# Start addresses of the fp32r operands in a decoder trunk: every one at a multiple of 64 bytes

## The chip, the cores and the metric

One core of one Trainium2 chip runs the whole program. The metric is the device time of one launch in microseconds. The kernel before takes 1127.47 us, the median of 3 runs (1127.37 to 1127.56).

## What is computed

A decoder trunk of two pre-RMSNorm layers on 512 tokens of width 1024, in float32. Cut to what matters here:

```
h = x
# layer 0
hn = rms_norm(h, mixer_norm_g[0])
q, k, v, g, u = split(hn @ w_in)              # 1024 -> 4 * 512 + 512
o = group_norm(retention(rope(q), rope(k), v))
h = h + concat([silu(g) * o, multiscale_pool(u)]) @ w_out
h = h + (silu(hf @ w_gate) * (hf @ w_up)) @ w_down     # hf = rms_norm(h), 1024 -> 2816 -> 1024
# layer 1
h = h + conformer_conv(rms_norm(h))           # 1024 -> 2 * 1024, GLU, causal conv of width 31,
                                              # LayerNorm, swish, 1024 -> 1024
h = h + swiglu(rms_norm(h))                   # as above
return rms_norm(h, final_norm_g)
```

## The kernel before, in words

The activations are kept feature major, as eight tiles of 128 features by 512 tokens. Every large product is made with three fp32r matmuls. Each operand is split into a part rounded to fp32r (the names end in h) and the exact rest (the names end in l), and `mm3` adds up high times high (L197), high times low (L198) and low times high (L199):

```
    def mm3(out, wh, wl, xh, xl, start, stop):
        nc.tensor.matmul(out, lhsT=wh, rhs=xh, start=start, stop=False)
        nc.tensor.matmul(out, lhsT=wh, rhs=xl, start=False, stop=False)
        nc.tensor.matmul(out, lhsT=wl, rhs=xh, start=False, stop=stop)
```

`lhsT` is the stationary operand, 128x128, loaded by a LDWEIGHTS of its own ahead of each matmul; `rhs` is the moving one, 128x512, or 128x256 where the tokens are worked in halves.

The weights come in 102 chunks of at most 128x2048 floats. `start_load` issues the transfer of a chunk to `wr`, and `split_load` makes `wh` on ScalarE (L179) and `wl` on VectorE (L182). Each of `wr`, `wh` and `wl` has two buffers, so chunk n+2 is written when TensorE is done with chunk n. `feature_major` runs over the eight feature tiles k of the input and over the two groups of 128 columns of a chunk, six matmuls for each k. `down` runs over the eleven hidden tiles f of half an FFN, three matmuls for each. For v and g (L446 to L448) the roles are exchanged: the activations are stationary and the weights move.

The stages on TensorE, with the name of the PSUM tile by which the profile knows each: `ps_qk`, `ps_u`, `ps_v`, `ps_g` (input projections), `ps_s` and `ps_o` (retention, in plain fp32), `ps_wo` (output projection), then `ps_gu` and `ps_dn` (the FFN's two products, each in two halves), `ps_pw` (the first product of the convolution module), `ps_c` (the convolution, plain fp32), `ps_p` (its last product; four small products of the pooling have that name too), and the second FFN. The last stage of the FFN, and parts of the convolution module, work in halves of 256 tokens.

The tiles lie in pools that are opened one after the other, and so their addresses in SBUF follow from the sizes of what was opened earlier: `const`, `res`, `wp` (weights), `xp` (the inputs `xgh`, `xgl` of `ps_gu` and `ps_pw`), `wk`, `sm` (small tiles, among them four for each tag of `rsqrt`, in two buffers), and, above all of them, one of `mx` (mixer), `hp` (hidden tiles `hh`, `hl` of an FFN) or `cx` and `cw` (convolution module). The first layer's inputs `xgh`, `xgl` lie in `mx`, as do `mh` and `ml`; `zh` and `zl` lie in `cx`.

Of the kernel before, what the change touches and what calls it, by code (L numbers as in the profile page):

```python
# [34 lines left out]
# columns of the per-channel vectors packed as [128, n]  # L35
# [8 lines left out]
# columns of the constants that depend on shapes alone  # L44
# [7 lines left out]
# 2*pi cut into parts: products with the rounded quotients are exact  # L52
# [5 lines left out]
def _parts(bits, n):  # L58
    # 2*pi to 120 bits
    num = 0x6487ED5110B4611A62633145C06E0E68  # L60
    den = 1 << 124
    out = []
    from fractions import Fraction
    rest = Fraction(num, den)
    for _ in range(n):
        e = 0
        while rest >= Fraction(2) ** (e + 1):
            e += 1
        while rest < Fraction(2) ** e:
            e -= 1  # L70
        unit = Fraction(2) ** (e - bits + 1)
        part = (rest // unit) * unit
        out.append(float(part))
        rest -= part
        if rest == 0:
            break
    return out
# [3 lines left out]
def trunk(ctx: ExitStack, tc: tile.TileContext, a: dict):  # L81
# [14 lines left out]
    vg = const.tile([P, KT], F32, name="vg")  # L96

# [15 lines left out]
    # TensorE's clock rises while it is busy: products of zeros until the first data arrive  # L113
# [6 lines left out]
    # ---------------------------------------------------------------- weights  # L120
# [16 lines left out]
    def start_load():  # L137
        """The transfer of the next chunk of weights."""
        i = state["started"]
        if i >= len(plan):  # L140
            return
        state["started"] += 1
        name, j, kt, c = plan[i]
        raw = wp.tile([P, CHUNK], F32, tag="wr", name=f"wr{i}", bufs=AHEAD + 1)
        if i == 0:
            # the first rows of x and of the weights arrive side by side
            for k in range(KT):
                s = slice(k * c, (k + 1) * c)
                nc.sync.dma_start(X[:, k, :], xT[k])
                nc.sync.dma_start(raw[:, s], a[name][j][:, s])  # L150
            nc.sync.dma_start(con, a["con"])
        else:
            pieces = 4 if i == 1 else 1
            step = kt * c // pieces
            for k in range(pieces):
                s = slice(k * step, (k + 1) * step)
                nc.sync.dma_start(raw[:, s], a[name][j][:, s])
        raws[i] = raw

    def split_load(pieces=1, apart=False):  # L160
        """The split of the next chunk of weights: one step per piece, or two."""
        i = state["next"]
        if i >= len(plan):
            return
        if i not in raws:
            start_load()
        state["next"] += 1
        name, j, kt, c = plan[i]
        n = kt * c
        raw = raws.pop(i)  # L170
        wh = wp.tile([P, CHUNK], F32R, tag="wh", name=f"wh{i}")
        wl = wp.tile([P, CHUNK], F32R, tag="wl", name=f"wl{i}")
        ready[(name, j)] = (wh[:, :n].rearrange("p (k c) -> p k c", c=c),
                            wl[:, :n].rearrange("p (k c) -> p k c", c=c))
        pieces = KT if i == 0 else 4 if i == 1 else pieces
        step = n // pieces
        for k in range(pieces):
            s = slice(k * step, (k + 1) * step)
            nc.scalar.copy(wh[:, s], raw[:, s])  # L179
            if apart:  # L180
                yield
            nc.vector.tensor_tensor(wl[:, s], raw[:, s], wh[:, s].bitcast(F32), ALU.subtract)  # L182
            if i == 0:
                norm_input(k, vg[:, k:k + 1], None, xin)
            yield
# [15 lines left out]
    def feature_major(ps, wh, wl, xh, xl, cols=FULL, between={}, ks=range(KT)):  # L201
        """ps[:, i] = the i-th 128 columns of the weights, transposed, times x; between: what else is issued, and when."""
        for k in ks:
            if k in between:
                between[k]()
            for i in range(2):
                c = slice(i * P, (i + 1) * P)
                mm3(ps[:, i, cols], wh[:, k, c], wl[:, k, c], xh[k][:, cols], xl[k][:, cols], k == 0, k == KT - 1)

    def high_first(ps, wh, wl, xh, xl, cols, ks):  # L210
        """feature_major, without xl as long as it can be."""
        for low in range(2):
            for k in ks:
                for i in range(2):
                    c = slice(i * P, (i + 1) * P)
                    o = ps[:, i, cols]
                    if low:
                        nc.tensor.matmul(o, lhsT=wh[:, k, c], rhs=xl[k][:, cols], start=False, stop=k == KT - 1)
                    else:
                        nc.tensor.matmul(o, lhsT=wh[:, k, c], rhs=xh[k][:, cols], start=k == 0, stop=False)  # L220
                        nc.tensor.matmul(o, lhsT=wl[:, k, c], rhs=xh[k][:, cols], start=False, stop=False)

    def split_scaled(h, l, src, scale):
        """h + l = src * scale, h rounded to 12 significant bits, l the exact rest."""
# [7 lines left out]
    # -------------------------------------------------------------- residual  # L232
# [7 lines left out]
    def norm_input(k, gain, acc, pool=None):  # L240
        """The split of X[k] * gain, and X[k]^2 added to acc."""
# [15 lines left out]
    def rsqrt(v, n, tag):  # L257
        """v ** -0.5 on [128, n], by Newton steps from the exponent's halving."""
        y = sm.tile([P, n], F32, tag=f"rs_y{tag}", name="rs_y")
        t = sm.tile([P, n], F32, tag=f"rs_t{tag}", name="rs_t")  # L260
        hv = sm.tile([P, n], F32, tag=f"rs_h{tag}", name="rs_h")
        half = sm.tile([P, n], I32, tag=f"rs_i{tag}", name="rs_i")
# [9 lines left out]
    def token_sums(acc, cols=FULL):  # L272
        """Sums over the partitions: [128 tokens, tiles of tokens]."""
# [7 lines left out]
    def spread(v, name, out=None):  # L281
        """[128 tokens, n] -> [128, 128 n], the same row on every partition."""
# [21 lines left out]
    def add_residual(j, ps, gain=None, acc=None, bias=None):  # L304
        """X of tiles 2j and 2j+1 += ps, then the next norm's input."""
# [18 lines left out]
    # ------------------------------------------------------- retention + pool  # L324
    def mixer():
        nonlocal xin
        with ExitStack() as m:
# [4 lines left out]
            # both halves of the partitions share the angles: one half of the tokens on each  # L332
# [18 lines left out]
            # rotary tables  # L351
# [11 lines left out]
            # the last rounding can leave the range by an ulp  # L363
# [12 lines left out]
            # q and k, rotated  # L376
# [27 lines left out]
            # pooling, feature major  # L404
            def pool_group(gi, ps):
# [5 lines left out]
                while d < w:  # L411
                    # columns before the first stay zero in u: windows reach back w - 1 at most
# [43 lines left out]
            # scores, transposed: [keys, queries]; heads' outputs token major  # L456
# [16 lines left out]
            # normalised in place of v  # L473
# [27 lines left out]
            # the pooled half of the output projection, then the gated heads, back to feature major  # L501
# [22 lines left out]
    # ------------------------------------------------------------------- FFN  # L524
# [4 lines left out]
    def ffn_in(layer, acc, gain, hp):  # L529
        nacc = None  # L530
        row = {}
        for half in range(2):
            hh, hl = [], []

            def hidden(ps):
# [5 lines left out]
                hh.append(hp.tile([P, S], F32R, tag="hh", name=f"hh{len(hh)}"))  # L541
                hl.append(hp.tile([P, S], F32R, tag="hl", name=f"hl{len(hl)}"))
# [30 lines left out]
    def finish(hh, hl, acc):  # L573
        """The last two tiles, and the last norm with the tokens on the partitions, in halves of the tokens."""
# [6 lines left out]
        def tail_add(i, cols):  # L581
            """The residual, its square and its product with the gain."""
# [7 lines left out]
        def turn(t, ks):  # L590
            """Tiles ks of x to rows of tokens."""
# [48 lines left out]
    # ------------------------------------------------------------------ conv  # L640
    def conv(acc):
        with ExitStack() as m:
# [12 lines left out]
            def gated(j, ps, cols, between=lambda: None):  # L655
                """u of tile j, after CW columns of zeros."""
# [13 lines left out]
                # R[32 q + c, i, t] = u[4 c + i, t + q]  # L670
                if j not in Rs:
                    Rs[j] = cw.tile([P, 4, 28 + S], F32, tag="R", name=f"R{j}")
                    # taps of 32 channels, four at a time, on the diagonals
# [31 lines left out]
            # Channels less a pivot, the mean of two of the tiles: their sums and those of their squares  # L705
            # give the mean and the variance, which the pivot's distance from the mean cannot swamp.
# [14 lines left out]
            def pivot_tile(j, ps, cols):  # L721
                """A convolved tile, with its bias and less the pivot, into the sums."""
# [8 lines left out]
            def stats(cols):  # L731
                """The mean less the pivot and the reciprocal deviation: [128 tokens, 2]."""
# [69 lines left out]
            # the last tiles and the norm in halves of the tokens: each engine's work in this order  # L802
# [85 lines left out]
def _chunks(w, cols, kt=None):  # L888
    """(K, M) -> [chunk, 128, kt * cols]: columns cut first, then rows."""
# [7 lines left out]
def _paired(a, b):  # L897
    """Columns of a and b, 128 of one beside 128 of the other."""
    K, M = a.shape
    return np.stack([a.reshape(K, M // P, P), b.reshape(K, M // P, P)], 2).reshape(K, 2 * M)  # L900
# [69 lines left out]
```

## Time and profile before

| | |
|---|---|
| median of 3 runs | 1127.47 us |
| span of the profiled execution, first to last instruction | 1125.3 us |
| TensorE (PE) busy | 1110.1 us, 99% |
| weight loads (PEld) busy | 896.5 us, 80% |
| VectorE (DVE) busy | 579.8 us, 52% |
| ScalarE (ACT) busy | 334.9 us, 30% |
| granted TensorE clock, mean | 0.997 |

The profiled execution has no device time of its own beside its span; 2.2 us of the median lie around the span. A profile's row gives engine, operation, output and inputs, shapes, and the number of instructions. A matmul's duration in these rows is longer than the distance from its start to the start of the next one, since matmuls overlap in the array; where this text speaks of a pitch, it means that distance from start to start. A timeline row begins with the start in microseconds and the duration.

### The profile page before, as it was taken

Reading aid. Unit: us, or ns where it says so; the run is one execution under the profiler, and the core shown is the slowest. Engines: PE = TensorE matmul, PEld = TensorE weight load, DVE = VectorE, ACT = ScalarE, POOL = GpSimd, SP = SyncE. Lnnn points to the kernel's source line nnn. Section 1 sums busy time; section 2 is a strip of 40 time slices with the busy share of each in tenths; the row PEclk is TensorE's granted clock in tenths of the full one; section 3 lists DMA queues with packets and bytes.
Section 4 is the critical chain, followed back from the end, with each engine's and each line's share of the span. In section 5 each row is a group of like instructions: output and inputs, shape, how many; then the busy total and the mean of one; then the engine's idle time right before and its main releaser. Section 6 shows DMA issues by size and latency. Waiting matters only on the chain.

```text
span 1125.3 us, 12874 instructions
## 1 busy us (share of the span) xinstructions
PE 1110.1 (99%) x5504; PEld 896.5 (80%) x5504; DVE 579.8 (52%) x784; ACT 334.9 (30%) x383; POOL 20.1 (2%) x10
## 2 busy tenths in 40 slices
PE   9999999999999999999999999999999999999996
PEld 6877778888888888888886577988888888888886
DVE  7876636453432343534569957854444324344333
ACT  6631134232221232323322124432322112222231
POOL 0000100000000000000000410000000000000000
PEclk9999999999999999999999999999999999999998
DMA  8322113222223323222427562233222232231212
GB/s 278 123 85 103 38 38 119 107 81 107 78 78 126 112 75 112 76 77 91 139 86 117 93 141 76 75 113 111 77 101 67 88 133 92 101 112 52 96 59 75
DMA packets 24744, 109.89 MB, mean 98 GB/s; under 512 B 2800, under 2 KB 6768, under 8 KB 15984
## 3 DMA queue, kind: packets, MB, share of 16 engines
q1 hardware_dynamic: 24112, 108.03, 29.7%
q8 instruction: 43, 0.70, 0.3%
q10 hardware_dynamic: 576, 1.05, 0.3%
q14 instruction: 13, 0.11, 0.0%
HBM read 100.34 MB, written 2.10 MB: 91 GB/s over the span
## 4 chain that ended last, share of the span: by engine, by line
PE 91%; DVE 6%; ACT 1%; DMA 1%; issue 1%; SPq 0%; DVEq 0%; ACTq 0%
PE ps_gu L197 14%; PE ps_gu L198 14%; PE ps_gu L199 14%; PE ps_dn L199 7%; PE ps_dn L198 7%; PE ps_dn L197 7%; DVE d L692 4%; PE ps_c L700 2%; PE ps_qk L198 1%; PE ps_qk L197 1%; PE ps_wo L198 1%; PE ps_qk L199 1%; PE ps_wo L199 1%; PE ps_wo L197 1%; PE ps_pw L197 1%; PE ps_pw L198 1%
## 5 line engine op out<-in xcount | busy, mean ns | idle before, releaser
L179 ACT CAST wh<-wr 128x2048 fp32r<-128x2048 f32 (+4 forms) x116 | 179.7, 1553 | 517.0 <-PE ps_gu L198 240.5
L197 PE MATMUL ps_gu<-xgh,wh 128*128 128x512 f32 x704 | 274.4, 390 | 0.0
L198 PE MATMUL ps_gu<-xgl,wh 128*128 128x512 f32 x704 | 273.9, 389 | 0.0
L199 PE MATMUL ps_gu<-xgh,wl 128*128 128x512 f32 x704 | 273.9, 389 | 0.0
L182 DVE TENSOR_TENSOR wl<-wr,wh 128x2048 fp32r<-128x2048 f32 (+4 forms) x116 | 214.1, 1849 | 104.5 <-ACT wh L179 104.2
L538 DVE TENSOR_TENSOR gu<-ps_gu,bc_rms 128x1024 f32<-128x1024 f32 x44 | 53.9, 1224 | 210.9 <-PE ps_gu L199 202.8
L199 PEld LDWEIGHTS ps_gu<-xgh,wl 128*128 128x128 f32 x704 | 132.1, 188 | 27.8
L197 PEld LDWEIGHTS ps_gu<-xgh,wh 128*128 128x128 f32 x704 | 132.1, 188 | 27.3
L198 PEld LDWEIGHTS ps_gu<-xgl,wh 128*128 128x128 f32 x704 | 132.2, 188 | 27.2
L199 PE MATMUL ps_dn<-hh,wl 128*128 128x512 f32 (+1 forms) x374 | 144.1, 385 | 0.0
L198 PE MATMUL ps_dn<-hl,wh 128*128 128x512 f32 (+1 forms) x374 | 142.4, 381 | 0.0
L197 PE MATMUL ps_dn<-hh,wh 128*128 128x512 f32 (+1 forms) x374 | 142.3, 380 | 0.0
L198 PEld LDWEIGHTS ps_dn<-hl,wh 128*128 128x128 f32 x374 | 70.3, 188 | 16.1
L197 PEld LDWEIGHTS ps_dn<-hh,wh 128*128 128x128 f32 x374 | 70.2, 188 | 14.9
L199 PEld LDWEIGHTS ps_dn<-hh,wl 128*128 128x128 f32 x374 | 70.2, 188 | 14.3
L197 PE MATMUL ps_pw<-xgh,wh 128*128 128x512 f32 (+1 forms) x160 | 56.3, 352 | 0.0
L229 ACT CAST hh<-act 128x512 fp32r<-128x512 f32 x44 | 27.3, 621 | 96.5 <-DVE act L540 96.5
L198 PE MATMUL ps_pw<-xgl,wh 128*128 128x512 f32 (+1 forms) x160 | 55.6, 347 | 0.0
L199 PE MATMUL ps_pw<-xgh,wl 128*128 128x512 f32 (+1 forms) x160 | 55.5, 347 | 0.0
L308 DVE TENSOR_TENSOR X<-ps_dn,X 128x1024 f32<-128x1024 f32 x15 | 18.4, 1225 | 69.7 <-PE ps_dn L199 69.7
L230 DVE TENSOR_TENSOR hl<-act,hh 128x512 fp32r<-128x512 f32 x44 | 30.5, 693 | 30.2 <-ACT hh L229 30.2
L700 PE MATMUL ps_c<-R,dg 128*32 128x512 f32 (+1 forms) x512 | 42.9, 487 | 2.3 <-ACT d L751 1.3
(188 smaller groups left out, 1184.7 us busy)
## 6 DMA issues: line engine op xcount, KB each, us to landing
wr<-in_w_gu SPq DMA_DIRECT2D x44, 1024.0 KB, 4.8
wr<-in_w_dn SPq DMA_DIRECT2D x32, 704.0 KB, 4.0
wr<-in_w_pw SPq DMA_DIRECT2D x12, 1024.0 KB, 4.9
R<-u SPq DMA_DIRECT2D x16, 270.0 KB, 8.5
wr<-in_w_o SPq DMA_DIRECT2D x4, 1024.0 KB, 4.7
X<-in_xT SPq DMA_DIRECT2D x8, 256.0 KB, 4.5
wr<-in_w_qk SPq DMA_DIRECT2D x2, 1024.0 KB, 5.4
wr<-in_w_u SPq DMA_DIRECT2D x2, 1024.0 KB, 4.8
```

Source lines behind the costliest of these rows:

```text
L179: nc.scalar.copy(wh[:, s], raw[:, s])
L182: nc.vector.tensor_tensor(wl[:, s], raw[:, s], wh[:, s].bitcast(F32), ALU.subtract)
L197: nc.tensor.matmul(out, lhsT=wh, rhs=xh, start=start, stop=False)
L198: nc.tensor.matmul(out, lhsT=wh, rhs=xl, start=False, stop=False)
L199: nc.tensor.matmul(out, lhsT=wl, rhs=xh, start=False, stop=stop)
L229: nc.scalar.copy(h, src)
L230: nc.vector.tensor_tensor(l, src, h.bitcast(F32), ALU.subtract)
L308: nc.vector.tensor_tensor(xx, ps, xx, ALU.add)
L538: nc.vector.tensor_tensor(t, ps, both(row["rb"]), ALU.mult)
L692: nc.vector.scalar_tensor_tensor(o, us[j][:, at], V("dwc", CW * j + q), o, ALU.mult, ALU.add)
L700: nc.tensor.matmul(ps[32 * i:32 * i + 32, :n], lhsT=dgs[j][:, i, g, :], rhs=Rs[j][:, i, 4 * g + cols.start:4 * g + cols.stop], start=g == ...
```

## The change

It alters where tiles lie, and nothing else. Tiles `wh` and `wl` become 64 bytes longer per partition, and so do the hidden tiles `hh` and `hl`, of which the first 512 columns are used as before. A 64-byte tile `pad` in `const` moves all later pools by 64 bytes. Four tiles of `rsqrt` have one buffer in place of two for the tag "b", and `rs_i` for "a4" too, which makes room and moves the pools above `sm`.

```diff
+ODD = 16
+PAD = 2
...
+    pad = const.tile([P, 8 * PAD], F32, name="pad") if PAD else None
...
-        wh = wp.tile([P, CHUNK], F32R, tag="wh", name=f"wh{i}")
-        wl = wp.tile([P, CHUNK], F32R, tag="wl", name=f"wl{i}")
+        wh = wp.tile([P, CHUNK + ODD], F32R, tag="wh", name=f"wh{i}")
+        wl = wp.tile([P, CHUNK + ODD], F32R, tag="wl", name=f"wl{i}")
...
-        y = sm.tile([P, n], F32, tag=f"rs_y{tag}", name="rs_y")
-        t = sm.tile([P, n], F32, tag=f"rs_t{tag}", name="rs_t")
-        hv = sm.tile([P, n], F32, tag=f"rs_h{tag}", name="rs_h")
-        half = sm.tile([P, n], I32, tag=f"rs_i{tag}", name="rs_i")
+        y = sm.tile([P, n], F32, tag=f"rs_y{tag}", bufs=1 if tag == "b" else 2, name="rs_y")
+        t = sm.tile([P, n], F32, tag=f"rs_t{tag}", bufs=1 if tag == "b" else 2, name="rs_t")
+        hv = sm.tile([P, n], F32, tag=f"rs_h{tag}", bufs=1 if tag == "b" else 2, name="rs_h")
+        half = sm.tile([P, n], I32, tag=f"rs_i{tag}", bufs=1 if tag in ("b", "a4") else 2, name="rs_i")
...
-                hh.append(hp.tile([P, S], F32R, tag="hh", name=f"hh{len(hh)}"))
-                hl.append(hp.tile([P, S], F32R, tag="hl", name=f"hl{len(hl)}"))
+                hh.append(hp.tile([P, S + ODD], F32R, tag="hh", name=f"hh{len(hh)}")[:, :S])
+                hl.append(hp.tile([P, S + ODD], F32R, tag="hl", name=f"hl{len(hl)}")[:, :S])
```

The instructions of every engine, their order and their waits are the same in both programs, row for row; line numbers grow by up to four. What differs is the addresses. From the programs as built, the start of each fp32r operand within its partition, modulo 128 bytes (the column and row steps inside a tile are multiples of 128 bytes, so one number stands for a whole tile):

| stage | fp32r matmuls of 512 columns | moving, before | stationary, before | moving, after | stationary, after |
|---|---|---|---|---|---|
| `ps_gu` | 2112 | 64 | 64 | 0 | 0 or 64 by chunk |
| `ps_pw` | 288 (and 192 of 256 columns) | 64 | 64 | 0 | 0 or 64 by chunk |
| `ps_dn` | 990 (and 132 of 256) | 32 | 64 | 64 or 0 by tile | 0 or 64 by chunk |
| `ps_p`, last product | 96 (and 192 of 256) | 32 | 64 | 64 | 0 or 64 by chunk |
| `ps_qk` and `ps_u` | 192 and 96 | 32 | 64 | 64 | 0 or 64 by chunk |
| `ps_wo` | 192 | 32, half of them 96 | 64 | 64, half of them 0 | 0 or 64 by chunk |
| `ps_v` and `ps_g` | 96 and 96 | 64 | 32 | 0 or 64 by chunk | 64 |
| `ps_p`, pooling | 12 | 96 | 96 | 0 | 0 |

So after the change about half of the 512-column matmuls have both operands at the same place modulo 128, and the other half have them 64 bytes apart. Pools `wp` and `xp` lie between 35,520 and 117,440 bytes, `mx`, `hp` and `cx` begin at 139,808 (before) or 139,840 (after).

## The prediction

> **What bounds the kernel now.** The page comes first: the engines' busy time, and the chain of work that ended last.
>
> ```profile
> span 1125.3 us, 12874 instructions
> ...
> PE 1110.1 (99%) x5504; PEld 896.5 (80%) x5504; DVE 579.8 (52%) x784; ACT 334.9 (30%) x383; POOL 20.1 (2%) x10
> ...
> PE 91%; DVE 6%; ACT 1%; DMA 1%; issue 1%; SPq 0%; DVEq 0%; ACTq 0%
> ```
>
> PE is busy nearly all the time and makes up 91% of the chain. "Busy" alone does not say that it works at its best, so the view of waits follows, for PE alone, and the busy time by stage, with the cuts laid where the product changes.
>
> ```profile
> PE ps_ms L278 <- DVE acc L761: 1.5, 1, 1.5
> ```
>
> ```profile
> 312.20:373.80 61.60, 61.60 (x266) 49.55 (x264) 19.74 (x14) 12.82 (x11) 0.00 (x0) 1.00 0.30 106
> 373.80:493.50 119.70, 119.70 (x529) 99.10 (x528) 50.96 (x42) 32.06 (x31) 0.00 (x0) 1.00 0.26 91
> ```
>
> The longest wait of PE on another engine is 1.5 us in the whole span (the view lists the longest first: total, times, longest one). In the FFN's stages (the two rows of the second view; columns are length, then PE, PEld, DVE, ACT, POOL) PE has no gap, the clock column reads 1.00, DVE is busy for 32% (19.74 of 61.60) and 43% (50.96 of 119.70). There only the pitch of the matmuls counts, the distance from one start to the next. The first row is one half of an FFN's `ps_dn`: 8 chunks of 33 matmuls, 264, in 61.60 us, 233.3 ns each. The second is `ps_gu`: 11 chunks of 48, 528, in 119.70 us, 226.7 ns each. (The counts in brackets take in neighbours that overlap an edge.) Same width, same clock, no wait, and 6.7 ns apart. The timeline of PE gives the pitch elsewhere, from the first and last row of a stretch without a gap:
>
> ```profile
> 724.63 0.39 PE L197 MATMUL ps_p<-zh,wh 128*128 128x512 f32 x1
> ...
> 735.83 0.39 PE L197 MATMUL ps_p<-zh,wh 128*128 128x512 f32 x1
> 39.78 0.40 PE L198 MATMUL ps_qk<-xgl,wh 128*128 128x512 f32 x1
> ...
> 50.28 0.40 PE L198 MATMUL ps_qk<-xgl,wh 128*128 128x512 f32 x1
> 53.78 0.40 PE L198 MATMUL ps_u<-xgl,wh 128*128 128x512 f32 x1
> ...
> 64.98 0.40 PE L198 MATMUL ps_u<-xgl,wh 128*128 128x512 f32 x1
> 169.83 0.40 PE L198 MATMUL ps_wo<-ml,wh 128*128 128x512 f32 x1
> ...
> 180.79 0.40 PE L197 MATMUL ps_wo<-mh,wh 128*128 128x512 f32 x1
> 125.80 0.39 PE L448 MATMUL ps_g<-wh,xgl 128*128 128x512 f32 x1
> ...
> 136.80 0.40 PE L447 MATMUL ps_g<-wl,xgh 128*128 128x512 f32 x1
> ```
>
> There are 48, 45, 48, 47 and 47 steps between the two rows of each pair: 233.3 ns for `ps_p`, `ps_qk` and `ps_u`, 233.2 for `ps_wo`, 234.0 for `ps_g`. So there are two classes, and the table of addresses sorts them without an exception. Where both operands begin at 64 modulo 128 (`ps_gu`, and `ps_pw`, which runs the same code as `ps_gu`), the pitch is 226.7. Where the moving operand lies at 32 or 96, or the stationary one at 32 (`ps_g`), it is 233.2 to 234.0. Code and shapes don't sort them: `ps_qk`, `ps_p` and `ps_gu` all come out of `feature_major` with the same steps, and the first layer's `xgh` in `mx` is slow where its namesake in `xp` is fast.
>
> Narrow matmuls show no difference. First `ps_pw` of 256 columns, all at 64, then `ps_dn` of 256, whose moving operand is at 32:
>
> ```profile
> 663.75 0.28 PE L198 MATMUL ps_pw<-xgl,wh 128*128 128x256 f32 x1
> ...
> 668.43 0.28 PE L198 MATMUL ps_pw<-xgl,wh 128*128 128x256 f32 x1
> 1099.74 0.28 PE L199 MATMUL ps_dn<-hh,wl 128*128 128x256 f32 x1
> ...
> 1102.86 0.28 PE L198 MATMUL ps_dn<-hl,wh 128*128 128x256 f32 x1
> ```
>
> 39 steps in 4.68 us and 26 in 3.12: 120.0 ns both. From this and 226.7, 256 more columns cost 106.7 ns, so 512 columns by themselves would take 213.3, and 13.3 ns of each aligned matmul are no streaming.
>
> **The change part by part.** The order and the waits are the same, so no term comes from a moved instruction. The counts, one row of each stage (its other two lines have as many):
>
> ```profile
> L197 PE MATMUL ps_gu<-xgh,wh 128*128 128x512 f32 x704 | 274.4, 390 | 0.0
> L197 PE MATMUL ps_dn<-hh,wh 128*128 128x512 f32 x330 | 129.4, 392 | 0.0
> L197 PE MATMUL ps_pw<-xgh,wh 128*128 128x512 f32 x96 | 37.7, 393 | 0.0
> L197 PE MATMUL ps_qk<-xgh,wh 128*128 128x512 f32 x64 | 25.7, 402 | 0.0
> L446 PE MATMUL ps_g<-wh,xgh 128*128 128x512 f32 x32 | 13.1, 411 | 0.0
> ```
>
> The 390 ns in the first row is not the pitch: a matmul's end lies behind the start of the next.
>
> 1. `ps_dn`: 990 x 6.67 ns = 6.60 us. I take 226.7 for the new pitch, the row of the only wide fp32r matmuls with both operands at multiples of 64.
> 2. `ps_p` of 512 columns, 96 x 6.67 = 0.64 us, and `ps_u`, 96 x 6.67 = 0.64 us.
> 3. `ps_wo`, 192 x 6.67 = 1.28 us. The short waits of its stage stay.
> 4. `ps_qk`: 192. The first chunk of 48 runs while x arrives and I count it at nothing; 144 x 6.67 = 0.96 us. All of them would be 1.28.
> 5. `ps_v` and `ps_g`: 192 x (234.0 - 226.7 = 7.3) = 1.41 us.
> 6. `ps_gu` and `ps_pw`, 2112 + 288 matmuls: 0. They were aligned to 64 and still are, but the moving operand goes from 64 to 0 modulo 128, and every second chunk has its operands 64 bytes apart. No row of this trace has that. From both sides: it cannot save more than the 13.3 ns that are no streaming, and a cost of as much again, 13.3, is my upper estimate, twice the 6.7 that a distance of 32 costs.
> 7. Matmuls of 256 columns, plain fp32 ones, the 12 of the pooling: 0, by the rows of 120.0 ns; the 12 are under 0.1 us at 6.7 ns each.
> 8. `rsqrt` with fewer buffers: 0. Its tiles are written and read on DVE, in order, and no wait is added.
>
> On the path all of this is PE's own time, so it counts in full as long as the next chunk comes in time. `ps_dn` is the tightest, 33 matmuls for a chunk, 7.70 us now and 7.48 after:
>
> ```profile
> L182 DVE TENSOR_TENSOR wl<-wr,wh 128x1408 fp32r<-128x1408 f32 x32 | 52.0, 1625 | 58.4 <-ACT wh L179 58.4
> ...
> L179 ACT CAST wh<-wr 128x1408 fp32r<-128x1408 f32 x32 | 44.0, 1374 | 178.0 <-PE ps_dn L198 122.4 <-PE ps_gu L198 47.9 <-issue 7.7
> ```
>
> ```profile
> wr<-in_w_dn SPq DMA_DIRECT2D x32, 704.0 KB, 4.0
> ```
>
> The transfer of 4.0 us, the rounding of 1.37 and the rest's 1.63 are steps of a pipeline, none near 7.48, and ScalarE waits for PE, not PE for it. That cover would have to shrink by over 4 us a chunk before a gap opened. With the 6.7 ns gone, nothing else is late.
>
> The sum: 6.60 + 0.64 + 0.64 + 1.28 + 0.96 + 1.41 = 11.53 us off the profiled span of 1125.3, 1113.8. The median of the runs, 1127.47, stands 2.2 us above that span, for what lies around it; with the same 2.2 the forecast is 1115.9.
>
> A rule of the Trainium skill speaks against term 5. "TensorE: Matmul & The Clock Gate", Part 2, step 1, says that PE has two independent SBUF read ports, and that loading the next weights takes no read bandwidth from the running matmul. By it a stationary operand's address could not show in the pitch while its load is hidden, and term 5 would be 0 (sum 10.1, 1117.3). The trace disagrees: the loads take as long in both stages,
>
> ```profile
> L197 PEld LDWEIGHTS ps_gu<-xgh,wh 128*128 128x128 f32 x704 | 132.1, 188 | 27.3
> L447 PEld LDWEIGHTS ps_g<-wl,xgh 128*128 128x128 f32 x32 | 6.0, 189 | 1.5
> ```
>
> 188 and 189 ns, hidden in 226.7 and 234.0, and yet `ps_g`, with its moving operand at 64 and only its stationary one at 32, is slow. I keep the term.
>
> **The rivals.**
>
> *A. Operands 64 bytes apart free each other.* `ps_g` shows that the two streams of reads affect one another, so part of the 13.3 ns may be reads that meet at the same place modulo 128, where every fast row of before has both operands. If the half of the 4158 wide fp32r matmuls that now has them apart lost 6.67 ns more, 2079 x 6.67 = 13.9 us would come on top: 1102.0. With all 13.3 ns gone, 27.7 us: 1088.2. Against it: the trace has no wide matmul under 226.7.
>
> *B. The distance is what costs.* 0 bytes apart is 226.7, 32 apart is 233.3 (either operand), 96 against 64 is 233.2. These rows fit "each operand off a multiple of 64" as well as "the operands apart". If 64 apart costs what 32 does, 1200 matmuls of `ps_gu` and `ps_pw` lose 6.67 (8.0 us) and half of the 11.53 us, 5.8, does not come: 1115.9 + 8.0 + 5.8 = 1129.7. If it grows with the distance, to 240.0, `ps_gu` and `ps_pw` lose 1200 x 13.33 = 16.0 us, and of the 1758 slow ones half gain and half lose 6.67: 1127.5 + 16.0 = 1143.5. This is the case on the other side: it decides from 11.53 us / 2079 = 5.5 ns per matmul 64 apart, and passes 0.2% slower, 2.25 us, at 6.6 ns. That bound of 0.2% is about what a measurement of this kernel can tell from no change. It ends on the slower side because more matmuls would leave the good place than reach it. Against it: a distance of 32 costs 0 in the narrow rows.
>
> *C. It is not the alignment.* Every slow stage has an operand in the pools above 139,808 bytes (`mx`, `hp`, `cx`), every fast one has both below. If the region matters, the change does nothing: 1127.5. Against it: `ps_g` and `ps_qk` come to nearly the same pitch with the operand up there in the other role, and no term in the trace depends on how far up it lies. A page bears on it: the Trainium skill's "SBUF — State Buffer", section "Door 1", speaks of 16-byte lines, and 32, 64 and 96 are all multiples of 16, so by that line size no operand gains by moving. The two classes of pitch do not look like it, unless C holds.
>
> *D. Only a part comes,* because the moving operand must be at 64 and not at 0 modulo 128, or the like: half of 11.53, 1121.7.
>
> **How the numbers follow.** The forecast, all alignment to 64 and nothing of 128, has 0.55: 1115.9. A has 0.16, D 0.05, C 0.10, B 0.14 (0.09 at 1129.7, 0.05 at 1143.5). Faster by over 0.2%: the forecast, A and D, 0.76. Within 0.2%: C and half of B's first value, 0.14. Slower: the rest of B, 0.10. The range goes from A's first value less a microsecond, 1101, to C plus one, 1128.5; left out are B and the far end of A, no more than 0.2.
>
> **What would show it.** In the profile after: a half of `ps_dn` takes 59.8 us in place of 61.60, 226.7 ns a matmul; a half of `ps_gu` still 119.7; wide matmuls of `ps_qk`, `ps_u`, `ps_wo`, `ps_p`, `ps_v`, `ps_g` all at 226.7; narrow ones at 120.0; PE's waits as they were. Wrong, and A or B, if pitches of neighbouring chunks of `ps_gu` differ, down or up; C if `ps_dn` stays at 233.3. A wait of PE for `wh` or `wl` in `ps_dn` would make the sum wrong though the pitches are right.

## The result, and the profile after

The changed kernel takes 1135.44 us (median of 4 runs, 1135.16 to 1135.84) against 1127.45 of the kernel before beside it. The ratio is 1.007, with a 95% interval of 1.0056 to 1.0084: slower, where 1115.9 was forecast. The profiled execution's span grew from 1125.3 to 1133.7 us.

The page of the kernel after, the same lines as before:

```profile
span 1133.7 us, 12874 instructions
...
PE 1119.6 (99%) x5504; PEld 897.8 (79%) x5504; DVE 579.9 (51%) x784; ACT 334.3 (29%) x383; POOL 19.7 (2%) x10
...
PE 95%; DVE 3%; ACT 1%; issue 1%; DMA 0%; SPq 0%; DVEq 0%; ACTq 0%
```

PE's busy time grew by 9.5 us and the others' stayed. The longest waits of PE show no new one:

```profile
PE ps_c L704 <- ACT d L755: 1.4, 1, 1.4
PE ps_idle L122 <- DVE zero L119: 1.2, 1, 1.2
```

So it is the pitch. The stages that were shown of before, a half of `ps_dn` and then a half of `ps_gu`, each cut at the start of its first matmul and of the next stage's first (length, PE busy, clock, share of DMA, GB/s):

```profile
314.07:375.37 61.30, 61.30 (x265) 1.00 0.30 106
375.37:497.66 122.29, 122.29 (x529) 1.00 0.26 89
```

`ps_dn` went from 61.60 to 61.30 us where 59.8 was forecast, 232.2 ns a matmul. `ps_gu`, which was to stay at 119.7, went to 122.29, 231.6 ns. There are two such halves of `ps_gu` in each FFN, +2.6 us for this one and about 10 us for all four; that is more than the whole loss. Two neighbouring chunks of `ps_gu`, of which the second has its weights in the other pair of buffers:

```profile
375.37:386.49 11.12, 11.12 (x49) 1.00 0.34 119
386.49:397.61 11.12, 11.12 (x50) 1.00 0.26 96
```

Both take 11.12 us for 48 matmuls. Rival B, as it was written, has one chunk at 226.7 and its neighbour slow; here both are slow by the same amount, though in one of them every operand begins at 0 modulo 128.

That is where the new theory came from. In the kernel before, the fast stages had more in common than the place modulo 128: their operands lay at the same place modulo 512 too, by the pool's sizes. In what follows, a distance is the start of a matmul's moving operand less that of its stationary one, in bytes, taken modulo 256 unless it is said otherwise; the starts are those of the built programs. Theory D (D for distance; it is not the prediction's rival D) says that the pitch depends on the distance alone. It began with a period of 512, and `scan32` brought it to 256. The kernel before has distance 0 in `ps_gu` and `ps_pw`, 96 in `ps_dn`, `ps_qk`, `ps_u`, the last product's `ps_p` and half of `ps_wo`, 32 in the other half, and 160 in `ps_v` and `ps_g`. The kernel after has, in `ps_gu`, 0 to `wh` and 128 to `wl` in one chunk, 192 and 64 in the next.

### The profile page after: what moved, and what is told of

Read it like the earlier page. It is cut to its first block, busy times and chain, and to the rows that moved or that the text cites. A ratio compares the mean times of both kernels' runs of the same rounds, so it can differ in the third digit from the quotient of the medians.

```text
span 1133.7 us, 12874 instructions
## 1 busy us (share of the span) xinstructions
PE 1119.6 (99%) x5504; PEld 897.8 (79%) x5504; DVE 579.9 (51%) x784; ACT 334.3 (29%) x383; POOL 19.7 (2%) x10
## 4 chain that ended last, share of the span: by engine, by line
PE 95%; DVE 3%; ACT 1%; issue 1%; DMA 0%; SPq 0%; DVEq 0%; ACTq 0%
PE ps_gu L203 14%; PE ps_gu L202 14%; PE ps_gu L201 14%; PE ps_dn L201 7%; PE ps_dn L203 7%; PE ps_dn L202 7%; PE ps_pw L201 2%; PE ps_pw L203 2%; PE ps_pw L202 2%; PE ps_c L704 2%; DVE d L696 2%; PE ps_wo L202 1%; PE ps_qk L202 1%; PE ps_wo L203 1%; PE ps_qk L203 1%; PE ps_qk L201 1%
## 5 line engine op out<-in xcount | busy, mean ns | idle before, releaser
L203 PE MATMUL ps_gu<-xgh,wl 128*128 128x512 f32 x704 | 278.8, 396 | 0.0
L202 PE MATMUL ps_gu<-xgl,wh 128*128 128x512 f32 x704 | 277.2, 394 | 0.0
```

## The experiments

The kernels are built on before, except `no_odd`. The first four ran on one chip, beside the same runs of before (1128.2 us).

**One place for all, `one_class`.** The pool `sm` is shrunk to 1536 bytes, and a tile of 320 bytes goes in ahead of `pwh`; all fp32r operands then begin at 192 modulo 512. Besides the smaller `rsqrt` tiles of the change:

```diff
-        v = sm.tile([P, NT], F32, tag="ms", name="ms")
+        v = sm.tile([P, NT], F32, tag="ms", name="ms", bufs=1)
...
-        v = sm.tile([P, 2], F32, tag="ms2", name="ms")
+        v = sm.tile([P, 2], F32, tag="ms2", name="ms", bufs=1)
...
+            mx.tile([P, 80], F32, name="mpad")
             pwh = mx.tile([P, 4, P], F32R, name="pwh")
```

> Before, with the pools shifted so that both operands of every fp32r matmul begin at 192 modulo 512. Theory D (the pitch is 226.7 ns when moving and stationary operand begin at the same place modulo 512, whatever that place is, and some 231 to 236 otherwise): every wide stage at 226.7, narrow ones at 120.0, about 1116 us. Theory S (same place modulo 128 is enough): the same, 1116. Theory R (the pools above 139,808 are slow by their region): ps_dn stays at 233.3, about 1127.

Measured: 1117.63 us, ratio 0.9902 (0.9887 to 0.9916). The windows of its profile, a half of `ps_dn` and a half of `ps_gu`:

```profile
309.02:368.86 59.84, 59.84 (x266) 1.00 0.32 108
368.86:488.54 119.68, 119.68 (x530) 1.00 0.26 91
```

Both are at 226.7 ns, and so is every other wide stage. Rival C, the region of SBUF, falls: by the program as built `hh` and `hl` begin 352 bytes lower than in before, still far above the weights. The gain that was forecast for the change, 11.5 us, is there (10.6), in a kernel that has the operands in one place, and not only at multiples of 64.

**The change without its padding, `no_odd`.**

```diff
-ODD = 16
+ODD = 0
```

> After, with ODD at 0: no padding of wh, wl, hh, hl; the shift by 64 and the smaller rsqrt tiles stay. All operands at multiples of 64; in ps_gu and ps_pw both at the same place modulo 512, in the other stages 64 apart. Theory D: ps_gu 226.7, ps_dn 230 to 234, about 1122 to 1128 us. Theory S: the same pitches, since 64 apart is another place modulo 128. The recorded forecast's theory (multiples of 64 are enough) would give 226.7 everywhere, 1116.

Measured: 1120.99 us, ratio 0.9933 (0.9918 to 0.9947), better than expected, since a distance of 64 turned out cheap:

```profile
310.36:370.81 60.45, 60.45 (x266) 1.00 0.31 107
370.81:490.54 119.73, 119.73 (x530) 1.00 0.26 91
```

`ps_dn` is at 229.0 ns, neither 226.7 nor 233.3, and `ps_gu` is back at 226.8. In other words, without `ODD` the change gains 7 us, and with it loses 8. Multiples of 64 alone don't give 226.7.

**All at 64 modulo 128, `upper_64`.**

```diff
     warm = sm.tile([P, 1], F32, tag="warm", name="warm", bufs=1)
+    sm.tile([P, 8], F32, tag="spad", name="spad", bufs=1)
```

> Before, with 32 bytes more in the pool sm, so that all operands begin at 64 modulo 128, but those above sm 128 bytes away from the weights modulo 512. Theory D: ps_gu 226.7, ps_dn 230 to 234, about 1122 to 1128 us. Theory S: every wide stage 226.7, about 1116.

Measured: 1126.97 us, ratio 0.9988 (0.9978 to 0.9997), 0.1% under before.

```profile
310.98:372.57 61.59, 61.59 (x265) 1.00 0.32 106
372.57:492.27 119.70, 119.70 (x530) 1.00 0.26 91
```

`ps_dn`, with both operands at 64 modulo 128 and 128 bytes apart, is as slow as it was with its moving operand at 32: 233.3. So it is neither the multiple of 64 nor the same place modulo 128.

**Everything moved together, `pad_alone`.**

```diff
     vg = const.tile([P, KT], F32, name="vg")
+    const.tile([P, 16], F32, name="pad")
```

> Before, with 64 bytes more in const: every operand moves by 64, and all distances stay. Theories D and S: as before, 1127.5 us, ps_gu 226.7 and ps_dn 233.3. Theory A64 (the moving operand must be at 64 and not at 0 modulo 128): ps_gu rises to about 231, some 1138.

Measured: 1127.94 us, ratio 0.9995 (0.9986 to 1.0005), no difference.

```profile
312.42:374.04 61.62, 61.62 (x266) 1.00 0.32 107
374.04:493.75 119.71, 119.71 (x529) 1.00 0.26 90
```

Every start has changed and no distance has, and no pitch moved. Where an operand begins does not matter by itself; A64, near to rival D, falls.

**The table, `scan32` and `scan16`.** The weights of each `ps_dn` chunk j are moved inside their tiles, which have room for it. In `scan32`, layer 1 also does every such chunk in halves of 256 columns. The line of the move:

```diff
+        oh = ol = 0
+        if name.startswith("w_dn"):
+            oh = ol = 8 * j
+        wh, wl = wh[:, oh:oh + n], wl[:, ol:ol + n]
```

That is `scan32` (offsets in floats of 4 bytes). `scan16` has in place of the middle two lines:

```diff
+        if name == "w_dn0":
+            oh = ol = 8 * j + 4
+        elif name == "w_dn1":
+            ol = 8 * j
```

> one_class, with the weights of chunk j of each layer's ps_dn moved by 32 j bytes inside their tiles, so that the distance of the moving operand from the stationary one takes 16 values in steps of 32; in layer 1 every such chunk is done in halves of 256 columns. Theory D: the pitch depends on the distance alone: 226.7 at 0, 228.8 at 64 (as in no_odd), 233.3 at 96, 128, 160 and 192. If the period is 256, as the rows of ps_wo in no_odd hint (226.7 at 256), the second 8 chunks repeat the first 8; if it is 512, they don't. Narrow: 120.0 at 0, 117.8 at 64, something down to 113 elsewhere. If the distance is not the cause, all chunks have one pitch.

> one_class, with the weights of chunk j of ps_dn in layer 0 moved by 32 j + 16 bytes, and in layer 1 the weights wl alone moved by 32 j bytes. Theory D: no distance that is an odd multiple of 16 is at 226.7, most near 233. In layer 1 only the matmuls that have wl as their stationary operand, or load it while they run, change; the triple's mean lies between 226.7 and the pitch of the same distance in scan32.

Both ran once, for their profiles; no time is compared. The chunks of layer 0 in `scan32`, 33 wide matmuls each, cut at their first starts; the distances in the order of the rows are 0, 224, 192, 160, 128, 96, 64 and 32, and in the last two rows 256 and 64, from the second half of the FFN:

```profile
308.49:315.97 7.48, 7.48 (x34) 1.00 0.29 96
315.97:323.67 7.70, 7.70 (x35) 1.00 0.28 94
323.67:331.37 7.70, 7.70 (x34) 1.00 0.31 97
331.37:339.09 7.72, 7.72 (x35) 1.00 0.30 93
339.09:346.76 7.67, 7.67 (x35) 1.00 0.28 94
346.76:354.46 7.70, 7.70 (x35) 1.00 0.41 136
354.46:362.02 7.56, 7.56 (x34) 1.00 0.38 141
362.02:369.73 7.71, 7.71 (x35) 1.00 0.34 107
489.41:496.89 7.48, 7.48 (x34) 1.00 0.30 96
535.38:542.94 7.56, 7.56 (x34) 1.00 0.41 141
```

256 gives 7.48 us, like 0, and 64 gives 7.56 both times, though the earlier of these two rows is at 320 when counted modulo 512. All eight chunks of the second half repeat those of the first to 0.01 us, so the period is 256 bytes. The narrow chunks of layer 1, 66 matmuls each, at 192, 160, 96 and 64:

```profile
879.20:886.68 7.48, 7.48 (x68) 1.00 0.30 97
886.68:894.61 7.93, 7.93 (x69) 1.00 0.28 93
902.43:910.35 7.92, 7.92 (x68) 1.00 0.37 134
910.35:918.12 7.77, 7.77 (x68) 1.00 0.34 135
```

From the starts inside the chunks, the median over stretches of six matmuls, in ns:

| distance | 0 | 32 | 64 | 96 | 128 | 160 | 192 | 224 |
|---|---|---|---|---|---|---|---|---|
| 512 columns | 226.7 | 233.3 | 228.8 | 233.3 | 232.6 | 234.2 | 233.3 | 233.3 |
| 256 columns | 120.0 | 117.7 | 117.8 | 120.0 | 118.8 | 120.0 | 113.3 | 118.2 |

`scan16` adds the odd multiples of 16. Here theory D's expectation was wrong in one point: 16 and 240 have the median of 0, 226.7 (over the whole chunk 16 comes to 227.4, some of its steps being longer); the others lie between 230.4 (80) and 233.4 over the whole chunk. In its layer 1, with `wl` alone displaced, the chunks at distances 0, 160 and 128 of `wl`:

```profile
861.36:868.84 7.48, 7.48 (x35) 1.00 0.30 96
884.17:891.84 7.67, 7.67 (x34) 1.00 0.30 94
891.84:899.47 7.63, 7.63 (x34) 1.00 0.28 94
```

The last one, `wh` at 0 and `wl` at 128, is what the changed kernel has in one of its two kinds of `ps_gu` chunk, the second of the two rows of 11.12 us above. Its pitch is 231.2 here (7.63 us for 33) and 231.5 there (11.114 us for 48, from the starts; the median of stretches is 231.2 in both). So displacing one of the two weights is enough to slow the group of three. The other kind, 192 and 64, was not tried by itself.

**A large dose, `all_160`.** The activations of all stages go to 160 from the weights.

```diff
+    xp.tile([P, 40], F32, tag="xpad", name="xpad")
     warm = sm.tile([P, 1], F32, tag="warm", name="warm", bufs=1)
```

> one_class, with a tile of 160 bytes ahead of the small tiles and behind the weights, so that all activations lie 160 bytes above the weights modulo 256, at multiples of 32. Theory D with the table of scan32: 234.2 ns for 160 and 233.3 for 96 (v and g, where the roles are exchanged), narrow ones 120.0 as before. 3966 x 7.5 + 192 x 6.7 = 31 us over one_class: 1148 to 1149 us, about 1.9% over before. If the starts matter and not the distance, ps_gu would stay near 226.7 or go to 233.3, with 1140 at the most.

Measured: 1145.35 us against 1128.35 of before beside it, ratio 1.015 (1.0133 to 1.0167).

```profile
316.33:378.19 61.86, 61.86 (x266) 1.00 0.31 106
378.19:501.88 123.69, 123.69 (x529) 1.00 0.25 88
```

234.3 ns in both, as the table says. The total is 3 us short of the expectation: its span is 28.5 us above that of `one_class`, not 31. Narrow matmuls ran at 117.3 to 118.3 (median of each chunk) instead of 120.0, so the lower row of the table does not carry over from `scan32`'s `ps_dn` to this kernel; and the convolution module, whose chain runs in part through VectorE, grew by 1.9 us only.

**Own operand or the one loaded beside it, `own_same`.** In `ps_dn` each hidden tile f and its 128 columns of weights are displaced together.

```diff
+STEP = {"w_dn0": 40, "w_dn1": 32}
...
+                o = len(hh) * STEP[f"w_dn{layer}"] % 64
-                hh.append(hp.tile([P, S], F32R, tag="hh", name=f"hh{len(hh)}"))
+                hh.append(hp.tile([P, S + 64], F32R, tag="hh", name=f"hh{len(hh)}")[:, o:o + S])
...
+            g = c + STEP[name]
+            h3, l3, r3 = [t[:, :kt * w].rearrange("p (k c) -> p k c", c=w)[:, :, :c]
+                          for t, w in ((wh, g), (wl, g), (raw, c))]
```

> one_class, with ps_dn laid out so that each hidden tile f, and the 128 columns of weights that belong to it, begin 160 f bytes (layer 0) or 128 f bytes (layer 1) further on modulo 256. A matmul's own two operands always begin at the same place; but at the last matmul of each three, the weights loaded meanwhile for the next f lie 160 or 128 away from the operand that is moving. If the distance between a matmul's own operands is what counts: 226.7 ns in both layers. If the distance between the moving operand and the weights loaded beside it counts: the mean of three rises, by the rows of scan16 with wl alone moved by 160 and 128, to somewhere between 228 and 232.

It ran once, for its profile. The first half of `ps_dn` in layer 0, and in layer 1:

```profile
309.47:370.75 61.28, 61.28 (x265) 1.00 0.31 107
862.99:923.63 60.64, 60.64 (x265) 1.00 0.31 107
```

232.1 and 229.7 ns, though no matmul has its own operands apart. Its own operands need not be apart, then, for a matmul to be slow; what lies beside it in the stream is enough. The weights loaded meanwhile are one such neighbour. The next moving operand is displaced in this kernel as well, so this run can't tell the two apart.

`scan16` says more, since in its layer 1 no moving operand is displaced, only `wl`. In the chunk with `wl` at 128 the mean distance to the next start is, by position in the three, 227.0, 232.6 and 234.0 ns (227.0, 226.0 and 227.0 in the chunk at 0). The second of the three has its own operands 0 apart, and the LDWEIGHTS of `wl` starts beside it; it loses 6.6 ns. `wl` gets into the array by that LDWEIGHTS alone, so a displaced load costs time without any displaced moving operand. The third has `wl` as its own operand and is slow as well. Whether its own distance costs it that, or the load before it, stays open.

**The best layout, `best`.** `one_class`, and the six chunks that are used in halves go 64 bytes on, to distance 192; `wh` and `wl` are 256 bytes longer for it, and `st`, `ag`, `var` and the `rsqrt` tiles "b" move from `sm` to `mx`.

```diff
+NARROW = {("w_pw1", 6), ("w_pw1", 7), ("w_pw2", 0), ("w_pw2", 1), ("w_dn1", 14), ("w_dn1", 15)}
...
+        if (name, j) in NARROW:
+            oh = ol = 16
```

> one_class, with the six weight chunks that are used in halves of 256 columns moved by 64 bytes, so that the moving operand of these 516 matmuls lies 192 bytes away modulo 256; some small tiles of the mixer are moved out of the pool sm to make room. Theory D: wide 226.7 everywhere, narrow 113.3 in place of 120.0: up to 516 x 6.7 = 3.4 us under one_class, 1114 to 1117.5 us, less where the last part of the convolution module waits for VectorE or a transfer.

Measured: 1115.97 us, ratio 0.9888 (0.9873 to 0.9903) to before, the fastest of all. Narrow matmuls of `ps_pw`, 37 steps:

```profile
659.67 0.28 PE L202 MATMUL ps_pw<-xgh,wh 128*128 128x256 f32 x1
...
663.86 0.28 PE L203 MATMUL ps_pw<-xgl,wh 128*128 128x256 f32 x1
```

113.2 ns. Of the 3.4 us, the span gained 1.6 over `one_class` (1113.4 against 1115.0): in `ps_p` and in one of the two `ps_dn` chunks most narrow matmuls ran at 117.8, though the distance is the same. The interval overlaps that of `one_class`, so this last step is not secured by the times, which were taken on two chips.

## Why the prediction was wrong, point by point

- **What bounds the kernel: right.** It is the matmul pitch in stages where PE never waits. No new wait came up, the order is the same, and the loss is in PE's busy time.
- **The two classes of pitch: right; their cause: the step that failed.** "The table of addresses sorts them without an exception" was true, but of a table modulo 128. In before, being at 64 modulo 128 and being 0 bytes apart modulo 256 went together in every wide stage, so the trace could not tell one from the other. `upper_64` tells them apart: with all at 64 and 128 bytes apart, `ps_dn` stays at 233.3; `one_class`, 0 apart, has 226.7 everywhere.
- **Terms 1 to 5, 11.53 us, on "226.7 for the new pitch, the row of the only wide fp32r matmuls with both operands at multiples of 64":** wrong. Those stages came to about 230 to 233 ns, by the mixture of distances, and `ps_dn` gained 0.3 us a half in place of 1.8. Where the distance is made 0, the sum holds: 10.6 of 11.5 us in `one_class`.
- **Term 6, "`ps_gu` and `ps_pw`: 0": wrong, and the larger error.** 2112 x 4.9 ns, some 10 us. Its bounds, 13.3 ns either way, held it. The account closes: by the starts in the two traces `ps_gu` takes 10.0 us more, wide `ps_pw` 0.9 more, `ps_dn` 1.1 less and all other fp32r matmuls 1.0 less, 8.8 in sum, where the span grew by 8.4.
- **Term 5, kept against a rule of the Trainium skill:** its size went the way of the other terms, but keeping it was right. The stationary operand's place does show in the pitch while its load is hidden. With `wl` alone displaced by 128 the mean of the three rises from 226.7 to 231.2, and the second of them is slow beside the load of `wl`. The rule of the Trainium skill ("TensorE: Matmul & The Clock Gate", Part 2, step 1), that loading the next weights takes nothing from the running matmul, is at odds with that. `own_same` fits it but adds no proof, since the moving operands change there too.
- **Term 7, "narrow matmuls show no difference":** true of the two rows shown, which lie at 0 and 96, and by chance both have 120.0. Over all the distances tried narrow matmuls take from 113.3 to 120.0, and in the changed kernel they gained 0.6 us.
- **Rival A:** wrong for wide matmuls, none of which has a pitch under 226.7 at any of the 16 distances tried. Narrow ones do fall from 120.0 to 113.3, at 192. Its room of 13.3 ns is itself in doubt, as the last section says.
- **Rival B had the right kind of cause, at 0.14,** and the result lies between its two values, 1129.7 and 1143.5. Its rows, 0, 32 and 96, don't order by size: 64 costs 2.2 ns and 128 costs 5.9. It counted by 128 where the period is 256, and so took half of the chunks for harmless, which they were not.
- **Rival C** fell with `one_class`. Rival D, as a rule on 64 and 0, fell with `pad_alone`.
- **The range** left out B as a whole, and that is where the time came to lie.

## What to carry to other kernels

Where two streams are read together, look at the difference of their addresses and not at each one's alignment, and read it modulo more than the unit you have in mind: a table modulo 128 hid a period of 256. For these fp32r matmuls of 512 columns, bring all operands to one place modulo 256, and pad buffers by multiples of 256 bytes or not at all; a padding of 64 to spread the buffers cost 1.3% here (1135.4 against 1121.0 without it). When a stage is fast, ask what it has in common with itself before moving it.

## What the runs showed of the hardware

- The pitch of wide fp32r matmuls takes values from 226.7 to 234.3 ns, by the distance of the operands modulo 256 bytes, where a whole stage has one distance. Distances 0, 16 and 240 are the fast ones, at 226.7. The distance fixes the pitch to about 1 ns and no better: 128 gives 232.4 in `scan32` (7.67 us for 33) and 233.3 in `upper_64`.
- With 256 columns the order is another one: 120.0 at 0 and 113.3 at 192. The distance does not settle it: at 192 some stretches run at 113.3 and others at 117.8 (`best`), and 160 gives 120.0 in `scan32` and 117.3 to 118.3 in `all_160`. What decides stays open.
- No wide pitch fell below 226.7 at any distance tried. That 13.3 ns of it are no streaming is not shown: the prediction got them from 120.0 for 256 columns, and with the 113.3 of `best`, half of 226.7, the same subtraction leaves nothing.
- The rows of LDWEIGHTS hardly show it: for `ps_gu` their means are 188 ns on all three lines in before, and 190, 188 and 188 in the changed kernel, while the pitch rose by 4.9. The pitch tells, the load's duration does not.
